# One hybrid trunk step on one core: eight buffers for the first modulation loads, layer 0's rotations stored from GpSimd's queue, and one of its four quarters of scan tables computed by GpSimd

## The chip, the cores and the metric

The kernel runs on one core of a Trainium2 chip. A core has five engines that each run their own list of instructions in order: TensorE (PE; its weight loads are shown apart as PEld), VectorE (DVE), ScalarE (ACT), GpSimd (POOL) and SyncE (SP). ACT, POOL and SP also issue DMA transfers (shown as ACTq, POOLq, SPq). An instruction waits for what it needs, and everything behind it on the same engine waits with it. The metric is the device time of one execution in microseconds (us); lower is better.

## The reference

The reference is one inference step of a two-layer trunk over 512 latent tokens and 128 context tokens, 1024 wide. Cut to what matters here:

```python
def trunk_layer(x, mod, p, ctx):
    shift1, scale1, gate1, shift2, scale2, gate2 = mod      # silu(cond) @ w_mod[l] + b_mod[l]
    h = modulate(x, shift1, scale1)                         # rms(x) * (1 + scale) + shift
    z = h @ p['w_in']
    u_ssm, c_q, ckv, k_rope, uv = split(z)
    y_a, h_re, h_im = mixer_ssm(u_ssm, h0_re, h0_im, p)     # S5 scan, both directions, 16 groups
    y_b = block_attention(q, k, v)                          # latent attention, 8 heads
    y_c = mixer_gmlp(uv, p)
    x = x + gate1 * merge_heads(y_a, y_b, y_c, p['w_out_norm'], p['w_out'])
    return x + gate2 * conv_ffn(modulate(x, shift2, scale2), p)

def ssm_direction(u, h0, ...):                              # one direction of mixer_ssm
    a_bar = exp(A * dt); b_bar = (a_bar - 1) / A * B
    h[t] = a_bar * h[t - 1] + b_bar * u[t]                  # complex, 64 states a group
    y[t] = real(C * h[t])
```

## The kernel before

The residual stream xT stays in SBUF, channels on the partitions, 642 token columns. Products of full precision are made of three passes: each weight tile is loaded raw, cast by ACT (whi, line 117) and its rest taken by DVE (wlo, line 118), and PE multiplies hi by hi, hi by lo and lo by hi.

At the start of layer 0, PE multiplies the condition by four blocks of w_mod (sixteen loads of 512 KB by SP, three shared buffers "raw", line 256; matmuls "mod", line 260). They give shift and scale. Then each half of the tokens is normalised and modulated (DVE nt L352 and hl L357, ACT hh L356) and multiplied by w_in ("win" and "wtok").

The scan is chunked by eight positions. It needs, for each layer and each of four quarters of the groups, tables in DRAM: WEd (state input), Qd (output), Wd (direct taps), and for all quarters together the rotations Td (powers of rho). `ssm_tables(l, q, ...)` computes a quarter: tiles B, Cr, CT, bb, bs, G, we, Q0, Q1, tm, with transposes and a tap product on PE and copies on ACT. `ssm_rotations` computes Td in parts of four columns, 42 element-wise products on GpSimd for a part (tile Tr, scratch tr). For layer 0 these run while norm and w_in run: rotations on GpSimd, four quarters of tables on DVE, all put in DRAM by SP's queue. For layer 1 both run on GpSimd during layer 0's FFN.

`scans` then goes over the quarters: `ssm_load` brings we, T, qt and tp back by GpSimd's queue; `ssm_quarter` makes E on PE and ACT, fills R on ACT (line 728), and on DVE does m = E*T (line 741), the scan H (749), m = H*T (751) and the states hq (758, 760) that PE multiplies by qt. The tiles E, R, m1, m2, H, T, we, qt, tp, hq and ys are single slots of the pool `ssm`; before the scans the rotations' tiles lie in the slots E, R, m1 and m2.

`params(l)` loads a layer's small vectors by GpSimd's queue, transposes them on PE (line 147, "pa") and copies them on DVE.

A scheduler that runs while the program is built fixes the order of each engine; nothing is reordered on the chip.

Of the kernel before, what the change touches and what calls it, by code (L numbers as in the profile page):

```python
# [10 lines left out]
F32 = mybir.dt.float32  # L11
# [8 lines left out]
D = 1024  # L20
# [3 lines left out]
NT = 642          # token columns: 512 latent, 2 zero, 128 context  # L24
CX = 514          # first context column
# [3 lines left out]
NS = 82           # scan slots per row  # L29
NC = 81           # chunk columns per row (64 latent, 1 gap, 16 context)  # L30

TOK = [0, 128, 256, 384, CX]     # first column of each token tile

# [14 lines left out]
class Trunk:  # L48
# [17 lines left out]
    def banks(self, pairs):  # L66
        """PSUM of one phase: six banks, as four single ones or two pairs of them."""
# [20 lines left out]
    # ---------------------------------------------------------------- helpers  # L88
    def complex_mul(self, eng, o_re, o_im, a_re, a_im, b_re, b_im, t):
        """o = a * b (o apart from a and b); t: two scratch APs of the result's shape."""  # L90
# [7 lines left out]
    def rsqrt(self, v, n):  # L98
        """v: [128, n] tile -> tile of 1/sqrt(v)."""
# [15 lines left out]
    def split(self, raw, hi, lo):  # L115
        """hi + lo == raw, each short enough for one float32r pass."""
        self.nc.scalar.copy(hi, raw)  # L117
        self.nc.vector.tensor_tensor(lo, raw, hi.bitcast(F32), op=OP.subtract)  # L118

    def wload(self, src, shape, pool=None, tags=("whi", "wlo"), bufs=5, into=None):  # L120
        """src: DRAM AP [128, a, b] (a*b <= 1024), or a list of (first index in a, AP)
        -> (hi, lo) views of that shape."""
# [22 lines left out]
    def tr(self, out, in_, k=128):  # L145
        """PE transpose of in_ ([k, m]) into out ([m, k])."""
        self.nc.tensor.transpose(out, in_, self.ident[:k, :k])

    # ---------------------------------------------------------------- constants and parameters
# [16 lines left out]
    def params(self, l):  # L166
        """Vectors of layer l with their index on the partitions."""
# [48 lines left out]
    def cond(self):  # L216
        """silu of both condition vectors, as 32-column stationary blocks."""
# [12 lines left out]
    def mod_blocks(self, l, blocks):  # L230
        """Blocks of 512 columns of the modulation of layer l; a generator of four steps a
        block and a last one."""
# [17 lines left out]
        for b in blocks:  # L250
            src = self.I["w_mod"][l, :, b * 512:(b + 1) * 512].rearrange("(k p) n -> p k n", p=128)
            ps = self.pz("mod")
            for kp in range(4):
                raw = self.wp.tile([128, 1024], F32, name=self.uid("raw"), tag="raw", bufs=3)
# [20 lines left out]
    # ---------------------------------------------------------------- residual in and out  # L275
# [32 lines left out]
    # ---------------------------------------------------------------- modulated norm  # L308
    def norm(self, pool, l, which, lo, hi, hh, hl):
        """The statistics at once; returns what does the rest."""  # L310
# [1437 lines left out]
```

## Time and profile before

| what | value |
|---|---|
| three runs | 1848.2, 1854.93, 1855.78 us (median 1854.93) |
| span of the profiled execution, first to last instruction | 1844.3 us |
| granted TensorE clock, mean over the span | 0.954 |
| PE busy | 1712.1 us, 93% |
| DVE busy | 1153.7 us, 63% |
| ACT busy | 680.5 us, 37% |
| GpSimd busy | 265.3 us, 14% |

The profiled execution's own time beside its span is not listed; the three timed runs lie 3.9 to 11.5 us above that span. Busy shares are means over very unlike stages: for most of the span PE is busy without a break, and in the first 270 us it is busy for 201.35.

### The profile page before, as it was taken

How to read it: one execution, taken by the hardware profiler on the slowest of the kernel's cores; microseconds unless marked ns; L12 is line 12 of the kernel's file. 1: busy time of each engine (PE TensorE's matmuls, PEld its weight loads, DVE VectorE, ACT ScalarE, POOL GpSimd, SP SyncE). 2: the span in 40 equal slices, each digit the busy share in tenths (PEclk: the TensorE clock that was granted, in tenths of full speed). 3: DMA queues.
4: the chain of work that ended last, by engine and by line, in shares of the span. 5: the costliest groups of instructions: out<-in, count | busy, mean ns of one | idle time of the engine just before them, and what ended most of it. 6: DMA issues, size and time to landing. Idle time of an engine off the chain costs nothing.

```text
span 1844.3 us, 28301 instructions
## 1 busy us (share of the span) xinstructions
PE 1712.1 (93%) x10864; PEld 1497.3 (81%) x10864; DVE 1153.7 (63%) x2461; ACT 680.5 (37%) x1210; POOL 265.3 (14%) x720
## 2 busy tenths in 40 slices
PE   6777889999999999999999988999989999999998
PEld 2665754559799899999998875455979999999998
DVE  5867784667764546466567578566777464655564
ACT  3342453532451414234244355353335132332241
POOL 3920300000024040439000120000000000000000
PEclk7886989999999999999999978999989999999999
DMA  7464534402433424134121633440222131321221
GB/s 222 135 163 123 140 110 159 138 1 69 126 119 100 151 65 126 54 98 125 54 89 66 159 107 105 156 141 1 69 69 92 32 107 44 94 82 45 81 81 58
DMA packets 201895, 182.44 MB, mean 99 GB/s; under 512 B 33438, under 2 KB 162780, under 8 KB 201760
## 3 DMA queue, kind: packets, MB, share of 16 engines
q1 hardware_dynamic: 182224, 163.57, 29.3%
q0 software_dynamic: 5104, 14.62, 2.7%
q10 hardware_dynamic: 14432, 2.44, 0.7%
q8 instruction: 86, 1.41, 0.3%
q14 instruction: 49, 0.40, 0.1%
HBM read 161.94 MB, written 18.64 MB: 98 GB/s over the span
## 4 chain that ended last, share of the span: by engine, by line
PE 74%; DVE 9%; DMA 8%; ACT 4%; POOL 3%; issue 2%; ACTq 0%; SPq 0%; DVEq 0%; POOLq 0%
PE up L141 11%; PE up L143 11%; PE up L142 11%; PE dn L142 5%; PE dn L141 5%; PE dn L143 5%; PE mod L260 4%; DMA raw<-w_mod 3%; PE o L1278 3%; PE wo L141 1%; PE wo L143 1%; PE wo L142 1%; PE s L1258 1%; PE mx L1239 1%; PE win L141 1%
## 5 line engine op out<-in xcount | busy, mean ns | idle before, releaser
L141 PE MATMUL up<-hh,whi 128*128 128x322 f32 x1408 | 436.5, 315 | 9.5 <-ACT hh L356 8.7
L142 PE MATMUL up<-hl,whi 128*128 128x322 f32 x1408 | 439.6, 313 | 2.1 <-DVE hl L357 1.9
L143 PE MATMUL up<-hh,wlo 128*128 128x322 f32 x1408 | 440.6, 314 | 0.4 <-DVE wlo L118 0.4
L141 PEld LDWEIGHTS up<-hh,whi 128*128 128x128 f32 x1408 | 266.2, 191 | 22.3 <-issue 11.0
L142 PEld LDWEIGHTS up<-hl,whi 128*128 128x128 f32 x1408 | 268.5, 191 | 2.9 <-DVE hl L357 2.9
L143 PEld LDWEIGHTS up<-hh,wlo 128*128 128x128 f32 x1408 | 267.9, 190 | 1.7 <-issue 1.0
L118 DVE TENSOR_TENSOR wlo<-raw,whi 128x1024 fp32r<-128x1024 f32 (+1 forms) x116 | 143.5, 1240 | 142.1 <-ACT whi L117 133.4
L142 PE MATMUL dn<-glo,dh 128*128 128x322 f32 (+1 forms) x704 | 217.7, 311 | 0.0
L143 PE MATMUL dn<-gh,dl 128*128 128x322 f32 (+1 forms) x704 | 217.4, 310 | 0.0
L141 PE MATMUL dn<-gh,dh 128*128 128x322 f32 (+1 forms) x704 | 208.8, 310 | 0.1
L1492 DVE SCALAR_TENSOR_TENSOR xT<-dn,mod,xT 128x320 f32<-128x320 f32 (+2 forms) x288 | 112.1, 435 | 129.9 <-PE dn L143 129.7
L117 ACT CAST whi<-raw 128x1024 fp32r<-128x1024 f32 (+1 forms) x116 | 120.4, 1041 | 157.1 <-PE up L142 63.9
L1523 ACT ACTIVATE cv<-up,prm,cw 128x321 f32<-128x321 f32 x88 | 54.2, 620 | 247.0 <-PE up L143 243.3
L143 PEld LDWEIGHTS dn<-gh,dl 128*128 128x128 f32 x704 | 132.9, 189 | 0.0
L142 PEld LDWEIGHTS dn<-glo,dh 128*128 128x128 f32 x704 | 132.7, 188 | 0.0
L141 PEld LDWEIGHTS dn<-gh,dh 128*128 128x128 f32 x704 | 130.3, 189 | 0.6 <-ACT gh L117 0.6
L260 PE MATMUL mod<-raw,sT 128*32 128x512 f32 x384 | 93.9, 672 | 20.1 <-DMA raw<-w_mod 17.2
L1524 DVE SCALAR_TENSOR_TENSOR cv<-up,cw,cv 128x320 f32<-128x320 f32 x88 | 48.3, 549 | 73.2 <-ACT cv L1523 73.0
L118 DVE TENSOR_TENSOR dl<-raw,dh 128x1024 fp32r<-128x1024 f32 x44 | 56.6, 1286 | 35.3 <-ACT dh L117 35.2
L1241 DVE TENSOR_REDUCE nml<-mx 128x1 f32<-128x640 f32 x64 | 51.1, 818 | 26.3 <-PE mx L1239 26.0
L117 ACT CAST dh<-raw 128x1024 fp32r<-128x1024 f32 x44 | 46.2, 1049 | 48.3 <-DMA raw<-ffn_w_down 44.9
L141 PE MATMUL wo<-yh,whi 128*128 128x322 f32 (+1 forms) x192 | 59.9, 317 | 1.8 <-ACT yh L117 1.0
(468 smaller groups left out, 3316.0 us busy)
## 6 DMA issues: line engine op xcount, KB each, us to landing
raw<-w_mod SPq DMA_DIRECT2D x96, 512.0 KB, 4.0
raw<-ffn_w_up SPq DMA_DIRECT2D x88, 512.0 KB, 4.0
raw<-ffn_w_down SPq DMA_DIRECT2D x44, 512.0 KB, 3.3
raw<-w_in SPq DMA_DIRECT2D x10, 512.0 KB, 4.8
WEd<-we SPq DMA_DIRECT2D x16, 256.0 KB, 2.1
Qd<-Q SPq DMA_DIRECT2D x32, 128.0 KB, 1.9
we<-WEd POOLq DMA_DIRECT2D x8, 512.0 KB, 4.1
qt<-Qd POOLq DMA_DIRECT2D x8, 512.0 KB, 5.0
```

Of the source, the lines that this page charges most:

```text
L117: self.nc.scalar.copy(hi, raw)
L118: self.nc.vector.tensor_tensor(lo, raw, hi.bitcast(F32), op=OP.subtract)
L141: mm(ps, wh, xh, start=start, stop=False)
L142: mm(ps, wh, xl, start=False, stop=False)
L143: mm(ps, wl, xh, start=False, stop=stop)
L260: nc.tensor.matmul(ps[c:c + 32, :], self.sT[:, k, :], rv[:, j, :], start=k < 4, stop=k >= 4)
L1239: mm(pb[:, o, :320], qh[i][:96, tt * 128:(tt + 1) * 128], kh[i][:96, o * 320:(o + 1) * 320], start=True, stop=True)
L1241: V.tensor_reduce(nm[:, tt:tt + 1], pb[:, :, :320], axis=AX.XY, op=OP.max, negate=True)
L1278: mm(pb[i * 64:(i + 1) * 64, 0], Vt[:, kt, 2 * p + i], Ps[i][kt], start=kt == 0, stop=kt == 4)
L1492: self.nc.vector.scalar_tensor_tensor(self.xT[:, m, a:b], po[:, a - lo:b - lo], self.modcol(l, gi, m, c), self.xT[:, m, a:b], op0=OP.mult, ...
L1523: A.activation(z[:, 0:321], po[:, 0:321], AF.Identity, bias=b, scale=c1)
L1524: V.scalar_tensor_tensor(z[:, 1:321], po[:, 0:320], c0, z[:, 1:321], op0=OP.mult, op1=OP.add)
```

## The change

1. The four modulation blocks ahead of layer 0 load into a pool of their own, `pre`, of eight buffers, instead of the three shared ones. The pool lies on the right side, where `params(0)` had its rows.
2. `params(1)` moves from right behind the modulation to just before layer 0's scans.
3. Quarters 0, 1, 2 of layer 0's tables stay on DVE. Quarter 3 is computed by GpSimd, in the slots that the scans use later (tm0 in E, tm1 in R, G in m1, we in m2, Q0 in H, Q1 in T, and so on). Its puts go by GpSimd's queue.
4. Layer 0's rotations are made in four parts one after the other, in one tile (slot hq) and one scratch tile (slot ys), behind the scan input; all Td stores go by GpSimd's queue. hq is allocated when the scans begin.
5. Layer 1's tables are put away by GpSimd's queue too, and its rotations are made in two parts of eight columns instead of four of four.

The diff, cut to its core:

```diff
-    def mod_blocks(self, l, blocks):
+    def mod_blocks(self, l, blocks, pool=None):
...
-                raw = self.wp.tile([128, 1024], F32, name=self.uid("raw"), tag="raw", bufs=3)
+                raw = (pool or self.wp).tile([128, 1024], F32, name=self.uid("raw"), tag="raw",
+                                             bufs=8 if pool else 3)
...
-    def ssm_tables(self, l, q, pool, E):
+    def ssm_tables(self, l, q, pool, E, tags={}, ps_of=None):
...
+        ps_of = ps_of or self.pz
+        put = nc.gpsimd if E is nc.gpsimd else nc.sync
...
-            return pool.tile(list(sh), F32, name=self.uid(s), tag=s, bufs=bufs)
+            return pool.tile(list(sh), F32, name=self.uid(s), tag=tags.get(s, s), bufs=bufs)
...
-            nc.sync.dma_start(out=self.WEd[l][q][:, d].rearrange("p e r n -> p (e r n)"), in_=we)
+            put.dma_start(out=self.WEd[l][q][:, d].rearrange("p e r n -> p (e r n)"), in_=we)
...
-                nc.sync.dma_start(out=self.Qd[l][q][:, d, h], in_=Qv[:, h, :, o:o + 128])
+                put.dma_start(out=self.Qd[l][q][:, d, h], in_=Qv[:, h, :, o:o + 128])
...
-                nc.sync.dma_start(out=self.Wd[l][q][:, :, gq].rearrange("j c n -> c j n"), in_=src)
+                put.dma_start(out=self.Wd[l][q][:, :, gq].rearrange("j c n -> c j n"), in_=src)
...
-    def ssm_rotations(self, l, pool, E, tags):
-        for d in range(2):
-            for g0 in (0, 4):
-                c0 = l * 16 + d * 8 + g0
-                T = pool.tile([128, 4, 2, NS], F32, name=self.uid("Tr"), tag=tags[g0 // 4], bufs=1)
-                tm = [pool.tile([128, 4 * 32], F32, name=self.uid("tr"), tag=tags[2 + i], bufs=1)
...
-                    nc.sync.dma_start(
-                        out=self.Td[l][g0 // 2 + q][:, d].rearrange("p e r n -> p (e r n)"),
+    def ssm_rotations(self, l, pool, E, parts, tags=("Tr", "tr")):
+        N = 16 // parts
+        for p0 in range(0, 16, N):
+            c0 = l * 16 + p0
+            T = pool.tile([128, N, 2, NS], F32, name=self.uid("Tr"), tag=tags[0], bufs=1)
+            tm = pool.tile([128, 2, N * 32], F32, name=self.uid("tr"), tag=tags[1], bufs=1)
...
+            for i in range(0, N, 2):
+                d, q = divmod(p0 + i, 8)
+                nc.gpsimd.dma_start(
+                    out=self.Td[l][q // 2][:, d].rearrange("p e r n -> p (e r n)"),
...
-        hq = ssm.tile([128, 2, 2, 2, NS], F32, name=self.uid("hq"), tag="hq")
         if l == 0:
-            self.ssm_rotations(0, ssm, nc.gpsimd, ("E", "R", "m1", "m2"))
...
         U = self.ssm_input(l, ssm, uT)
+        if l == 0:
+            tags = {"tm0": "E", "tm1": "R", "G": "m1", "we": "m2", "Q0": "H", "Q1": "T",
+                    "B": "we", "Cr": "qt", "CT": "tp", "bb": "bbg", "bs": "bsg"}
+            for q in (3,):
+                self.ssm_tables(0, q, ssm, nc.gpsimd, tags, lambda s: self.pb(s)[:, 0])
+            self.ssm_rotations(0, ssm, nc.gpsimd, 4, ("hq", "ys"))
 
         def scans(tables):
+            hq = ssm.tile([128, 2, 2, 2, NS], F32, name=self.uid("hq"), tag="hq")
...
-            for q in range(4):
+            for q in (0, 1, 2):
                 self.ssm_tables(0, q, tb, V)
             tb_ctx.close()
+            self.params(1)
             scans(None)
...
-            mix = self.begin_layer(0, self.mod_blocks(0, (2, 0, 3, 1)))
-            self.params(1)
+            with tc.tile_pool(name="pre", bufs=1, side="right") as pre:
+                mix = self.begin_layer(0, self.mod_blocks(0, (2, 0, 3, 1), pre))
...
-                    hooks[4] = [lambda: self.ssm_rotations(l + 1, tb[0], nc.gpsimd,
-                                                           ("T0", "T1", "tm0", "tm1"))]
+                    hooks[4] = [lambda: self.ssm_rotations(l + 1, tb[0], nc.gpsimd, 2)]
```

The scheduler draws each engine's order anew. Three places matter later.

SP, the start, before: the first modulation loads stand right behind the loads of x.

```order
8 L283 DMA raw_396<-x_prompt 128x1024
9 L256 DMA raw_423<-w_mod 128x2x512
10 L256 DMA raw_427<-w_mod 128x2x512
11 L256 DMA raw_431<-w_mod 128x2x512
```

SP, the same place, of the change:

```order
8 L284 DMA raw_396<-x_prompt 128x1024
9 L134 DMA raw_685<-w_in 128x8x128
10 L134 DMA raw_692<-w_in 128x8x128
11 L886 DMA raw_823<-w_in 128x2x288
12 L257 DMA raw_426<-w_mod 128x2x512
13 L257 DMA raw_430<-w_mod 128x2x512
```

Three loads of w_in now stand ahead of the first of w_mod, and that first one waits until PE has transposed the rows of `params(0)`, because its buffer lies where they were.

ACT, end of the second half's norm, before: the fill of R for the first scan (two rows, slot R still holding a rotation part) stands between the norm's last hh.

```order
104 L356 ACTIVATE hh_415<-nt_985,mod_91 128x192
105 L356 ACTIVATE hh_415<-nt_989,mod_91 128x128
106 L728 COPY R_2029<-r_266 128x328 x2
107 L356 ACTIVATE hh_415<-nt_993,mod_91 128x192
108 L356 ACTIVATE hh_415<-nt_997,mod_91 128x128
```

ACT, of the change, where R is filled now: 66 rows behind the norm's last hh, beside the gMLP's scaling of v (line 1106) and the tap copies of quarter 3 (we_1081) and quarter 2 (we_1949).

```order
188 L1106 ACTIVATE v_1386<-v_1386,rs_y_240_1540 128x256 x5
189 L598 COPY we_1912<-we_1907 128x512
190 L731 COPY R_2029<-r_266 128x328 x2
191 L637 COPY we_1081<-tap_1060 128x240
192 L637 COPY we_1949<-tap_1928 128x240
193 L720 COPY E_2005<-e_2006 128x4x81
```

So no hh stands behind the fill of R any more.

POOL, of the change, the end of quarter 3 (Q_198) and the fourth rotation part (Tr_1232), the loads tp, T and we of the scans among them, and the first row of `params(1)`:

```order
242 L611 TENSOR_TENSOR Q_198_1047<-tm_188_986,tm_189_987 64x288 x2
243 L696 DMA tp_2003<-Wd_295 128x512
...
257 L95 TENSOR_TENSOR Tr_1232<-Tr_1232,tr_1233 128x4x8
258 L692 DMA T_1999<-Td_287 128x656
...
262 L646 DMA Wd_298<-we_1081 16x8x128 x4
...
267 L174 MEMSET rows_1960 13x128
...
299 L95 TENSOR_TENSOR Tr_1232<-Tr_1232,tr_1233 128x4x18
300 L96 TENSOR_TENSOR Tr_1232<-Tr_1232,tr_1233 128x4x18
301 L668 DMA Td_289<-Tr_1232 128x328
```

Before, GpSimd had nothing but memsets, small copies and loads behind the rotations; now quarter 3, four Wd puts and ten loads of `params(1)` (between rows 267 and 280) stand there as well, and the last Td store is row 302.

DVE, of the change, ahead of the first scan: the finish of quarter 3's taps (we_1081), the gMLP's gate (gt, yc) and quarter 2's taps (we_1949), then the scan's first product.

```order
346 L638 SCALAR_TENSOR_TENSOR we_1081<-id_80,dcol_1058,we_1081 128x16
347 L1113 TENSOR_TENSOR gt_1557<-gm_1555,gvb_339 128x320
...
351 L638 SCALAR_TENSOR_TENSOR we_1949<-id_80,dcol_1926,we_1949 128x16
...
356 L744 TENSOR_TENSOR m_320_2036<-E_2005,T_1999 128x656
```

Row 346 needs the tap product that PE makes of GpSimd's Q_198; before, the taps of all quarters came from DVE's own tables.

## Rows read from the trace of the kernel before

**Rows 1.** Windows: stretch, us, busy (count) PE PEld DVE ACT POOL, PEclk, DMA share, GB/s.

```profile
640.00:680.00 40.00, 40.00 (x296) 39.63 (x295) 17.95 (x38) 7.96 (x15) 22.19 (x42) 1.00 0.33 92
...
sum 400.00, PE 399.48 PEld 389.57 DVE 219.90 ACT 130.60 POOL 129.75; mean PE 39.95 PEld 38.96 DVE 21.99 ACT 13.06 POOL 12.98
```

**Rows 2.** Windows of the first 170 us by stage.

```profile
20.00:55.00 35.00, 26.35 (x95) 6.86 (x93) 27.68 (x147) 8.57 (x17) 12.93 (x51) 0.64 0.74 239
55.00:80.00 25.00, 17.84 (x110) 17.14 (x109) 21.03 (x53) 12.40 (x24) 25.00 (x80) 0.80 0.49 138
...
99.70:109.10 9.40, 1.31 (x8) 0.82 (x7) 0.28 (x2) 1.22 (x4) 3.72 (x15) 0.67 0.42 119
109.10:138.00 28.90, 25.16 (x205) 24.12 (x205) 21.81 (x72) 15.09 (x49) 1.30 (x4) 0.91 0.73 185
138.00:170.00 32.00, 23.74 (x167) 18.50 (x167) 25.19 (x70) 9.75 (x27) 0.84 (x4) 0.69 0.48 130
```

**Rows 3.** Timeline from 99.4 us: start, length, what [idle before <-releaser].

```profile
107.88 0.46 ACT L728 COPY R<-r 128x328 f32<-128x328 f32 x1 [11.19 <-DMA Td<-Tr]
...
109.10 0.42 DVE L357 SCALAR_TENSOR_TENSOR hl<-nt,mod,hh 128x192 fp32r<-128x192 f32 x1 [9.12 <-ACT hh L356]
...
109.12 0.61 PE L899 MATMUL wtok<-wth,hh 128*128 128x288 f32 x1 [8.11 <-ACT hh L356]
```

**Rows 4.** The chain that ended last, one piece: start, us, what.

```profile
102.94 4.85 DMA Td<-Tr
```

**Rows 5.** SP's timeline at the start: sixteen issues in a row.

```profile
14.44 35.88 SPq L256 DMA_DIRECT2D raw<-w_mod  x16
```

**Rows 6.** Windows: a stretch while w_mod streams.

```profile
26.00:32.00 6.00, 3.35 (x9) 0.37 (x9) 4.26 (x18) 2.73 (x6) 0.29 (x1) 0.65 0.86 282
```

**Rows 7.** DVE's timeline: the first product of the first half's norm.

```profile
54.81 0.54 DVE L352 SCALAR_TENSOR_TENSOR nt<-xT,mod,nbc 128x320 f32<-128x320 f32 x1
```

**Rows 8.** DVE's groups, 54 to 73.5 us: count, busy us, mean ns, idle before.

```profile
L118 DVE TENSOR_TENSOR wtl<-raw,wth 128x576 fp32r<-128x576 f32 x4 | 3.0, 746 | 0.0
L118 DVE TENSOR_TENSOR wlo<-raw,whi 128x1024 fp32r<-128x1024 f32 x2 | 2.6, 1278 | 0.0
```

**Rows 9.** DVE's groups, 110 to 170 us.

```profile
L608 DVE TENSOR_TENSOR Q<-tm,tm 64x288 f32<-64x288 f32 x24 | 10.8, 452 | 0.6
L604 DVE TENSOR_TENSOR tm<-pw,CT 128x288 f32<-128x288 f32 x12 | 5.4, 454 | 1.3 <-ACT CT L554 1.1
L605 DVE TENSOR_TENSOR tm<-pw,CT 128x288 f32<-128x288 f32 x12 | 5.4, 451 | 0.0
...
L92 DVE TENSOR_TENSOR tm<-pw,bb 128x256 f32<-128x256 f32 x6 | 2.5, 421 | 0.0
```

**Rows 10.** DVE's timeline: last table row, the first scan's product, its states.

```profile
169.76 0.24 DVE L635 SCALAR_TENSOR_TENSOR we<-id,dcol,we 128x16 f32<-128x16 f32 x1 [4.91 <-ACT we L634]
170.29 0.84 DVE L741 TENSOR_TENSOR m<-E,T 128x656 f32<-128x656 f32 x1 [0.29 <-POOL E L724]
...
180.21 1.13 DVE L758 TENSOR_TENSOR hq<-m 64x164 f32<-64x164 f32 x4
```

**Rows 11.** GpSimd's timeline: first and last of the four parts' 168 products.

```profile
47.64 0.24 POOL L91 TENSOR_TENSOR Tr<-Tr,rho 128x4 f32<-128x4 f32 x1
...
102.20 0.32 POOL L96 TENSOR_TENSOR Tr<-Tr,tr 128x72 f32<-128x72 f32 x1
```

**Rows 12.** GpSimd in layer 0's FFN: the same product of two successive parts.

```profile
828.32 0.20 POOL L92 TENSOR_TENSOR tr<-Tr,rho 128x4 f32<-128x4 f32 x1
...
837.54 0.21 POOL L92 TENSOR_TENSOR tr<-Tr,rho 128x4 f32<-128x4 f32 x1
```

**Rows 13.** GpSimd's timeline: one DMA issue.

```profile
127.44 0.54 POOL L693 DMA_DIRECT2D tp<-Wd  x1 [16.92 <-DMA Qd<-Q]
```

**Rows 14.** DVE's groups, 73 to 99 us, beside GpSimd's rotations.

```profile
L608 DVE TENSOR_TENSOR Q<-tm,tm 64x288 f32<-64x288 f32 x8 | 3.8, 479 | 0.2
```

More of the change, by code (lines that the diff above doesn't have):

```diff
@@ L550, in ssm_tables @@
                         in_=I["ssm_c_" + nm][l, d, g:g + 2].rearrange("g c p -> (g c) p"))
-        ps = self.pz("ct")
+        ps = ps_of("ct")
         self.tr(ps[:, :128], Cr)
@@ L588, in ssm_tables @@
                              [v4(x, 8) for x in tm])
-            ps = self.pz("we")
+            ps = ps_of("we")
             for e in range(2):
@@ L613, in ssm_tables @@
             for h in range(2):
-                nc.sync.dma_start(out=self.Qd[l][q][:, d, h], in_=Qv[:, h, :, o:o + 128])
+                put.dma_start(out=self.Qd[l][q][:, d, h], in_=Qv[:, h, :, o:o + 128])
         dcol = t("dcol", [128, 1])
         nc.gpsimd.memset(dcol, 0.0)
-        ps = self.pz("tap")
+        ps = ps_of("tap")
         for h in range(2):
@@ L642, in ssm_tables @@
                               ap=[list(src.ap[0]), [-16, 8], [1, 128]])
-                nc.sync.dma_start(out=self.Wd[l][q][:, :, gq].rearrange("j c n -> c j n"), in_=src)
-    def ssm_rotations(self, l, pool, E, tags):
+                put.dma_start(out=self.Wd[l][q][:, :, gq].rearrange("j c n -> c j n"), in_=src)
+    def ssm_rotations(self, l, pool, E, parts, tags=("Tr", "tr")):
         nc = self.nc
-        for d in range(2):
-            for g0 in (0, 4):
-                c0 = l * 16 + d * 8 + g0
-                T = pool.tile([128, 4, 2, NS], F32, name=self.uid("Tr"), tag=tags[g0 // 4], bufs=1)
-                tm = [pool.tile([128, 4 * 32], F32, name=self.uid("tr"), tag=tags[2 + i], bufs=1)
-                      for i in range(2)]
-                nc.gpsimd.memset(T[:, :, 0, 0:1], 1.0)
-                nc.gpsimd.memset(T[:, :, 1, 0:1], 0.0)
-                for j in range(7):
-                    b = 1 << j
-                    n = min(b, NS - b)
-                    sh = [128, 4, n]
-                    r_re, r_im = (bc(self.rho[:, j, r, c0:c0 + 4, None], sh) for r in range(2))
-                    x = [a[:, :4 * n].rearrange("p (g n) -> p g n", g=4) for a in tm]
-                    self.complex_mul(E, T[:, :, 0, b:b + n], T[:, :, 1, b:b + n],
-                                     T[:, :, 0, 0:n], T[:, :, 1, 0:n], r_re, r_im, x)
-                for q in range(2):
-                    nc.sync.dma_start(
-                        out=self.Td[l][g0 // 2 + q][:, d].rearrange("p e r n -> p (e r n)"),
-                        in_=T[:, 2 * q:2 * q + 2].rearrange("p e r n -> p (e r n)"))
@@ new lines, in ssm_rotations @@
+        N = 16 // parts
[3 more added lines that the diff above has]
+            tm = pool.tile([128, 2, N * 32], F32, name=self.uid("tr"), tag=tags[1], bufs=1)
+            nc.gpsimd.memset(T[:, :, 0, 0:1], 1.0)
+            nc.gpsimd.memset(T[:, :, 1, 0:1], 0.0)
+            for j in range(7):
+                b = 1 << j
+                n = min(b, NS - b)
+                sh = [128, N, n]
+                r_re, r_im = (bc(self.rho[:, j, r, c0:c0 + N, None], sh) for r in range(2))
+                x = [tm[:, i, :N * n].rearrange("p (g n) -> p g n", g=N) for i in range(2)]
+                self.complex_mul(E, T[:, :, 0, b:b + n], T[:, :, 1, b:b + n],
+                                 T[:, :, 0, 0:n], T[:, :, 1, 0:n], r_re, r_im, x)
+            for i in range(0, N, 2):
+                d, q = divmod(p0 + i, 8)
+                nc.gpsimd.dma_start(
+                    out=self.Td[l][q // 2][:, d].rearrange("p e r n -> p (e r n)"),
+                    in_=T[:, i:i + 2].rearrange("p e r n -> p (e r n)"))
```

## The prediction, made before the change was run

> **What bounds the kernel now.** I read the busy times by stage first, then the idle times and their releasers, then the chain that ended last. In layer 0's FFN, where layer 1's tables and rotations are made, PE is busy for 399.48 of 400 us [rows 1]: what GpSimd and its queue do there lies beneath PE, so the change's part for layer 1 is costed at nothing. Its cover is large: the tables are needed only when layer 1 begins, and GpSimd is busy for 129.75 of those 400 us.
>
> The time to be had lies in the first 180 us. From 20 to 55 us the sixteen modulation loads set the pace, from 55 to 80 DVE and GpSimd share the work, and from 99.7 to 109.1 nearly everything stands still: in 9.4 us PE works for 1.31 and DVE for 0.28 [rows 2]. The timeline says why. ACT's fill of R waited 11.19 us for Td<-Tr, since R's slot held a rotation part that had to be stored first; the norm's last hh stood behind it, and DVE waited 9.12 us and PE 8.11 us for that [rows 3]. The store itself is on the chain with 4.85 us [rows 4]. From 109.1 to 170 us DVE is busy for 47.0 of 60.9 us and PE for 48.9, at a granted clock that falls from 0.91 to 0.69 [rows 2]: neither engine is full, they wait for each other.
>
> **The change part by part.**
>
> *Modulation loads.* Before, they are issued from 14.44 to 50.3 us [rows 5]. Now three w_in loads (2 x 512 KB and 288 KB, 1.34 MB) go ahead and the first w_mod waits for the transposes of params(0). The fastest rate that the trace shows here is 282 GB/s [rows 6], the mean 239 [rows 2]; I take 250. The three loads are 5.4 us at that, so w_mod begins at about 20. Sixteen loads (8.39 MB) and three more of w_in between them (0.88 MB) take 33 to 39 us, 37 at 250: the last lands at 53 to 59 us, I take 57. Before, the norm could begin at 54.81 [rows 7]. More buffers thus do not end the modulation earlier: they keep the queue full, but the queue also carries w_in. What they bring comes later: the lower parts of w_in, 3.0 and 2.6 us of DVE [rows 8], no longer stand inside the first half's norm. Gain: 5.6 less 2 to 3, so 3 us (0 to 6).
>
> *The stall.* R is now filled behind all hh, so its 9.4 us go; I take 9. What hides the new fill is quarter 3 on GpSimd, whose scratch lies in R; that wait is costed below.
>
> *A quarter of tables off DVE.* On DVE it is 8 Q at 452 ns, 8 tm at 453 and 12 products for G at about 420 [rows 9]: 3.6 + 3.6 + 5.0 = 12.2 us, and small ones. Of 109.1 to 170 us, DVE's 47.0 would become 35. PE's 48.9 us there would be 25.16 x 0.91 + 23.74 x 0.69 = 39 at full clock, so this stage cannot shrink by more than about 15; at nothing, if PE sets it at its old clock. I take 12, as the quarter's own chain (tables, transposes, copies, store) goes with its work.
>
> Without GpSimd the sum is 3 + 9 + 12 = 24 us: the first scan's states, now at 180.21 [rows 10], would start at 156.
>
> *GpSimd.* It begins when the modulation's buffers are free, at about 58 us instead of 47.64 [rows 11]. Ahead of its row 242 (the end of quarter 3) stand 3.1 rotation parts, the quarter, 14 DMA issues, three waits for a part's stores before its tile is written again, and waits for PE and ACT. A part takes 54.9 / 4 = 13.7 us beside a busy DVE [rows 11] and 9.2 in the FFN [rows 12]; I take 12.5, nearer to the first, since DVE is as busy here. A quarter is 22.2 us in the FFN [rows 1]; with the parts' ratio (1.49) it would be 33; I take 26.6. An issue is 0.54 us [rows 13]. So: 39 + 26.6 + 7.6 + 5 for the stores + 5 for the other waits = 83 us (60 to 97), and row 242 is done at 141. DVE's row 346, and behind it the gMLP's gate and the scan's product, wait for the taps that PE makes of it. Then 23 more issues (12.4 us; ten are params(1), whose first memset waits for quarter 2's last puts), the rest of the fourth part (9), memsets (2) and the landing of the last stores (2): 25.5 us. The states hq, whose slot held the rotations, can be written at 166.5. That is later than the 156 that DVE and PE alone would need, so GpSimd decides: 180.2 - 166.5 = 13.7, say 14 us. The bounds: at 60 us of work the 24 stands (30 with every upper end), at 97 the gain is nothing.
>
> The scans, attention and everything behind are the same work, so the 14 us reach the end. On the profiled span that is 1844.3 - 14 = 1830.3; the median of the runs is 10.6 above that span, and I keep that: 1854.93 - 14 = 1841 us.
>
> *GpSimd beside DVE.* With GpSimd's rotations beside it, a Q product on DVE took 479 ns [rows 14], and 452 without [rows 9]: 6%, at most 2 us over the stretch, left out of the sum. GpSimd pays far more, 13.7 against 9.2. The Trainium skill, page "SBUF — State Buffer", section "Who interferes with whom", speaks against the change: a VectorE instruction with two SBUF inputs and a GpSimd instruction that reads SBUF lock each other out for a whole instruction. In this trace nearly all of that falls on GpSimd; the rule taken evenly is the third rival below.
>
> **The rivals.**
>
> 1. *GpSimd is hidden* (0.22). Row 242 comes before 130 us and DVE and PE set the time: 24 us, 1831. For it: parts at 9.2 as in the FFN. Against: DVE was nowhere idle while the parts took 13.7.
>
> 2. *GpSimd ends too late; slower* (0.14). The place is DVE's row 346, the wait for quarter 3's taps, with the gate and the scan behind it, and then hq. It decides when row 242 is done after 180.2 - 25.5 = 154.7 us, that is when GpSimd needs 97 us and not 83. Parts at 13.7 (42.5), the quarter at 33, issues 7.6, stores 6 and 15 of other waits are 104 us: row 242 at 162, hq at 188, 8 us late: 1863. For it: GpSimd, ACT and PE hand quarter 3 back and forth, and each is in order.
>
> 3. *DVE is held up by GpSimd* (0.12). If each of some 60 products with two inputs in SBUF (about half of the 53 and 72 that rows 2 count for two of the stretches) lost half of a GpSimd product (0.25 us), DVE would be 15 us longer and the gain 24 - 15 = 9: 1846. Against it: rows 14.
>
> 4. *The gain is given back* (0.14). The scans' loads stand in GpSimd's queue among rotations and params(1), and DVE's copies of params(1) stand between the scan and hq; if these and the later modulation cost what the stall gave, some 4 us remain: 1851.
>
> My forecast (GpSimd decides, but earlier than now; 0.38) has its own range of 1832 to 1853.
>
> **How the numbers follow.** A measurement of this kernel can tell about 0.5% (9.3 us) from no change. Faster by more: 0.30 of the forecast's 0.38, rival 1 and half of rival 3, 0.58. Within 0.5%: the forecast's rest (0.08), half of rival 3, 0.12 of rival 4 and 0.02 of rival 2, 0.28. Slower: 0.14. The range, 1824 to 1862, holds rival 1 with its upper bounds (30 us) and most of rival 2's near side; it leaves out about 0.13.
>
> **What would show it.** Right: no idle time of DVE before an hl near 100 us; R's fill waiting for GpSimd and nothing behind it that the norm needs; the first nt within 53 to 59 us and no wlo or wtl inside the first half's norm; DVE idle before the taps of quarter 3 or the states with GpSimd or its DMA as releaser; GpSimd busy without a break from 58 to about 165 us; the FFN as long as before. Wrong: the first scan's product waiting for nothing of GpSimd's (rival 1), hq after 180 us (rival 2), Q products on DVE above 600 ns (rival 3), or hq early and attention beginning no earlier than before (rival 4).

## The result, and the profile after

The changed kernel takes 1831.07 us (median of 4 runs, 1829.74 to 1833.83) against 1851.57 for the kernel before (4 runs, 1845.65 to 1855.78): a ratio of 0.989, interval 0.9864 to 0.9916. That is 20.5 us less; the forecast was 14 less. The profiled span fell by 14.3 us, from 1844.3 to 1830.0. That this is the 14 of the sum is chance, as the last experiment below shows: the first profile of the kernel before fell on a quick execution.

Busy times by stage, the stretches of [rows 2]:

```profile
20.00:55.00 35.00, 23.21 (x92) 6.11 (x93) 33.01 (x155) 13.71 (x29) 1.96 (x14) 0.80 0.89 303
55.00:80.00 25.00, 23.66 (x156) 22.56 (x154) 19.64 (x52) 10.57 (x28) 24.75 (x82) 0.93 0.12 24
99.70:109.10 9.40, 6.18 (x51) 5.78 (x49) 9.27 (x12) 3.23 (x8) 9.39 (x17) 1.00 0.82 215
109.10:138.00 28.90, 17.73 (x132) 16.03 (x132) 23.90 (x58) 10.24 (x29) 22.83 (x45) 0.77 0.69 183
138.00:170.00 32.00, 30.37 (x266) 26.40 (x266) 24.85 (x50) 14.72 (x37) 26.39 (x67) 0.94 0.53 149
```

The columns are those of [rows 2]: stretch, us, busy (count) of PE, PEld, DVE, ACT and POOL, PEclk (the granted TensorE clock), DMA share, GB/s. From 20 to 55 us the transfers run at 303 GB/s instead of 239, and DVE is nearly full: busy for 33.01 of 35 us, against 27.68. From 55 to 80 PE works 23.66 us instead of 17.84. The standstill from 99.7 to 109.1 is gone: DVE is busy for 9.27 of 9.4 us, GpSimd for 9.39.

SP's timeline at the start, where [rows 5] had sixteen loads of w_mod in one row:

```profile
13.78 3.88 SPq L134 DMA_DIRECT2D raw<-w_in  x2
18.91 0.37 SPq L886 DMA_DIRECT2D raw<-w_in  x1
19.65 12.97 SPq L257 DMA_DIRECT2D raw<-w_mod  x10
...
35.87 3.75 SPq L257 DMA_DIRECT2D raw<-w_mod  x4
```

The first w_mod is issued at 19.65, as forecast (20), the last by 39.6 instead of 50.3.

DVE's timeline: first and last product of the norm, the last table row (of quarter 2), the scan's product m and its states, for [rows 7, 10]:

```profile
53.48 0.99 DVE L353 SCALAR_TENSOR_TENSOR nt<-xT,mod,nbc 128x320 f32<-128x320 f32 x2
...
94.41 0.34 DVE L358 SCALAR_TENSOR_TENSOR hl<-nt,mod,hh 128x128 fp32r<-128x128 f32 x1
...
147.49 0.32 DVE L638 SCALAR_TENSOR_TENSOR we<-id,dcol,we 128x16 f32<-128x16 f32 x1 [0.24 <-ACT we L637]
...
152.47 0.84 DVE L744 TENSOR_TENSOR m<-E,T 128x656 f32<-128x656 f32 x1 [1.32 <-POOL E L727]
...
173.31 0.32 DVE L761 TENSOR_TENSOR hq<-m 64x164 f32<-64x164 f32 x1 [2.19 <-DMA Td<-Tr]
```

m comes 17.8 us earlier than before, hq only 6.9. The states wait 2.19 us for the rotations' last store, as forecast; m itself waits 1.32 us for GpSimd's copy into E.

GpSimd's timeline: its first rotation product, the end of quarter 3 (row 242), the waits behind it, the last stores, for [rows 11]:

```profile
53.47 0.20 POOL L91 TENSOR_TENSOR Tr<-Tr,rho 128x4 f32<-128x4 f32 x1
...
138.22 1.85 POOL L611 TENSOR_TENSOR Q<-tm,tm 64x288 f32<-64x288 f32 x2
...
147.43 0.59 POOL L692 DMA_DIRECT2D T<-Td  x1 [2.56 <-PE tap L635]
...
154.03 0.20 POOL L174 MEMSET rows<- 13x128 f32 x1 [1.59 <-DMA Wd<-we]
...
168.07 1.15 POOL L668 DMA_DIRECT2D Td<-Tr  x2 [0.30 <-POOL Tr L96]
```

DVE's groups, 73 to 152 us, for [rows 9, 14]; count, busy us, mean ns:

```profile
L611 DVE TENSOR_TENSOR Q<-tm,tm 64x288 f32<-64x288 f32 x24 | 13.8, 575 | 0.6
L608 DVE TENSOR_TENSOR tm<-pw,CT 128x288 f32<-128x288 f32 x12 | 7.2, 600 | 0.0
L607 DVE TENSOR_TENSOR tm<-pw,CT 128x288 f32<-128x288 f32 x12 | 7.0, 581 | 1.1 <-ACT CT L557 1.1
L94 DVE TENSOR_TENSOR tm<-pw,bb 128x256 f32<-128x256 f32 x5 | 5.0, 991 | 0.0
```

The same products took 452, 451, 454 and about 420 ns before. The means hide how the time is lost. DVE's view of the tiles tm and Q over the same stretch gives the shortest, the median and the longest in ns:

```profile
L611 DVE TENSOR_TENSOR Q<-tm,tm x24: 445/461/1021, 76.7 to 143.4; 64x288 f32<-64x288 f32 x24
L94 DVE TENSOR_TENSOR tm<-pw,bb x5: 418/434/3152, 82.5 to 136.9; 128x256 f32<-128x256 f32 x5
```

Most products are as quick as before. The mean of 991 ns comes from one product of 3.15 us among five. It began at 105.66, and four products of quarter 3 ran on GpSimd under it, one right after the other. Ten more table products took 0.85 to 1.25 us each, all begun between 109 and 139 us, while GpSimd worked on quarter 3.

### The profile page after: what moved, and what is told of

Same layout as the page of the kernel before. It is cut to its first block, busy times and chain, and to the rows that moved or that the text cites. A ratio compares the mean times of both kernels' runs of the same rounds, so it can differ in the third digit from the quotient of the medians.

```text
span 1830.0 us, 28203 instructions
## 1 busy us (share of the span) xinstructions
PE 1708.6 (93%) x10864; PEld 1499.7 (82%) x10864; DVE 1158.5 (63%) x2421; ACT 681.7 (37%) x1210; POOL 311.4 (17%) x738
## 4 chain that ended last, share of the span: by engine, by line
PE 75%; DVE 10%; DMA 8%; ACT 4%; issue 2%; POOL 1%; ACTq 1%; DVEq 0%; POOLq 0%
PE up L141 11%; PE up L143 11%; PE up L142 10%; PE dn L142 5%; PE dn L143 5%; PE dn L141 5%; PE mod L261 3%; DMA raw<-w_mod 3%; PE o L1287 3%; PE wo L141 1%; PE wo L143 1%; PE wo L142 1%; DVE wlo L118 1%; DMA raw<-ffn_w_up 1%; PE s L1267 1%
## 5 line engine op out<-in xcount | busy, mean ns | idle before, releaser
L118 DVE TENSOR_TENSOR wlo<-raw,whi 128x1024 fp32r<-128x1024 f32 (+1 forms) x116 | 147.4, 1272 | 155.2 <-ACT whi L117 146.5
L141 PE MATMUL dn<-gh,dh 128*128 128x322 f32 (+1 forms) x704 | 208.9, 310 | 2.3 <-DVE xT L1501 1.5
L261 PE MATMUL mod<-raw,sT 128*32 128x512 f32 x384 | 89.7, 642 | 21.7 <-DMA raw<-w_mod 19.8
```

The costliest lines, as they stand in the source:

```text
L141: mm(ps, wh, xh, start=start, stop=False)
L261: nc.tensor.matmul(ps[c:c + 32, :], self.sT[:, k, :], rv[:, j, :], start=k < 4, stop=k >= 4)
```

## The experiments

Two questions: which part of the change brings the gain, and does GpSimd decide through the states hq, as the prediction has it, or does the time follow something earlier, the scan's first product m, whatever hq does (the rival)? A third theory, that DVE pays for GpSimd's quarter, is told from both by the durations of DVE's own products. The diffs are cut to their core.

The times of all kernels, with four moments of their profiles: v, ACT's last copy of the gMLP's input out of PE's wtok (line 947 of the changed kernel); m, the scan's first product; hq, its first states; wo, PE's first matmul of layer 0's output projection. Medians of 4 to 12 runs each, ratio to the kernel before on the same chip; that kernel's medians there lie between 1851.57 and 1855.13, so that a difference of medians in us can be off by some 3.

| kernel | v | m | hq | wo | wo - m | wo - hq | median | ratio (interval) |
|---|---|---|---|---|---|---|---|---|
| before | 131.7 | 170.3 | 180.2 | 398.0 | 227.7 | 217.8 | 1851.57 | 1 |
| before, profiled again | 134.2 | 172.2 | 182.1 | 403.2 | 231.1 | 221.1 | 1852.85 | 1.0004 (0.9984 to 1.0024) |
| after | 124.9 | 152.5 | 173.3 | 382.2 | 229.8 | 208.9 | 1831.07 | 0.989 (0.9864 to 0.9916) |
| 1 eight buffers alone | 124.7 | 186.8 | 196.7 | 416.2 | 229.4 | 219.5 | 1871.1 | 1.0097 (1.0066 to 1.0128) |
| 2 rotation slots alone | 137.7 | 169.3 | 178.9 | 403.2 | 233.9 | 224.3 | 1855.98 | 1.0021 (1.0003 to 1.0039) |
| 3 quarter 3 on DVE | 118.2 | 160.8 | 170.5 | 392.9 | 232.1 | 222.4 | 1837.24 | 0.9919 (0.9892 to 0.9947) |
| 4 params(1) early | 132.4 | 183.6 | 194.2 | 409.5 | 225.9 | 215.3 | 1866.09 | 1.0088 (1.0056 to 1.0121) |
| 5 three buffers | 127.1 | 166.5 | 173.6 | 392.9 | 226.4 | 219.3 | 1845.57 | 0.997 (0.9954 to 0.9986) |
| 6 own slot | 145.1 | 152.7 | 160.9 | 387.2 | 234.5 | 226.3 | 1839.76 | 0.9953 (0.9933 to 0.9973) |
| 7 buffers, late params(1) | 133.6 | 168.3 | 178.3 | 397.8 | 229.5 | 219.5 | 1854.27 | 1.0018 (1.0 to 1.0036) |
| 8 params(1) behind the mixers | 124.5 | 152.8 | 164.9 | 386.0 | 233.2 | 221.1 | 1833.43 | 0.9899 (0.9873 to 0.9925) |
| 9 U behind w_in | 132.6 | 172.5 | 182.5 | 403.1 | 230.6 | 220.6 | 1857.64 | 1.0009 (0.999 to 1.0028) |
| 10 short rotations | 118.5 | 141.4 | 150.8 | 370.9 | 229.5 | 220.1 | 1825.84 | 0.9841 (0.9816 to 0.9865) |
| 11 two parts | 150.2 | 164.5 | 171.4 | 395.3 | 230.8 | 223.9 | 1844.83 | 0.9943 (0.9921 to 0.9964) |

**1. Eight buffers alone.** The kernel before with the pool `pre` and nothing else; params(1) stays right behind the modulation.

```diff
...
-            mix = self.begin_layer(0, self.mod_blocks(0, (2, 0, 3, 1)))
+            with tc.tile_pool(name="pre", bufs=1, side="right") as pre:
+                mix = self.begin_layer(0, self.mod_blocks(0, (2, 0, 3, 1), pre))
             self.params(1)
```

> The kernel before with only the eight modulation buffers. Theory A (the steps of the prediction): w_in's lower parts leave the first half's norm, the second half's norm begins about 8 us earlier (68.7 against 77.1 us in the changed kernel), but the rotations still lie in the scan's slots and DVE still computes four quarters; and the order drawn here also has R's fill behind the norm, so that the stall should be gone too: 8 to 14 us faster, 1838 to 1844. Theory B (the quarter on GpSimd and the rotations' slots bring nearly all): at most 4 us faster, 1848 or more.

It was slower by about 1%: theory A is out, and theory B names no loss. GpSimd's timeline, then the waits (total, times, longest), 53 to 80 us:

```profile
61.51 0.20 POOL L174 MEMSET rows<- 13x128 f32 x1 [3.88 <-PE mod L261]
```

```profile
POOL uT L868 <- PE pa L147: 10.2, 1, 10.2
...
DVE cw L198 <- PE pa L147: 4.6, 1, 4.6
...
PE pa L147 <- DMA rows<-q_norm: 3.4, 1, 3.4
```

The rows of params(1) get the memory of `pre`, so their memset waits for the last modulation matmul, ten loads follow, and PE, DVE and GpSimd wait for these in the middle of the first norm.

**2. Rotation slots alone.** The kernel before with the rotations of parts 4 and 5 of the change: those of layer 0 in hq and ys, those of layer 1 in two parts, Td stored by GpSimd's queue. Layer 0's are still written ahead of the scan input, and layer 1's tables still go by SP's queue.

```diff
...
-            self.ssm_rotations(0, ssm, nc.gpsimd, ("E", "R", "m1", "m2"))
+            self.ssm_rotations(0, ssm, nc.gpsimd, 4, ("hq", "ys"))
...
```

> The kernel before with only the rotations moved: one tile in hq's slot, four parts one after the other, stores by GpSimd's queue; three buffers, four quarters on DVE. Theory A: the stall of 9.4 us before 109 us goes, and nothing else changes: 7 to 10 us faster, 1842 to 1845. Theory B (the stall only hid other waits: DVE's four quarters set the time up to the first scan): under 4 us faster.

The stall is gone (the norm ends at 100.0 us, not 110.2), yet m stays at 169.3 and the time is not shorter. SP's timeline, then the waits from 100 to 170 us:

```profile
108.64 8.07 SPq L677 DMA_DIRECT2D U<-Ud  x8
117.13 0.39 SPq L884 DMA_DIRECT2D raw<-w_in  x1
```

```profile
PE wtok L899 <- DVE wtl L118: 8.2, 2, 4.5
```

The last w_in load of line 884 stands behind the eight U loads in SP's queue, and PE waits for it. Experiment 9 takes this cover away.

**3. Quarter 3 on DVE.** The changed kernel with all four quarters on DVE: buffers, rotations and the late params(1) stay.

```diff
-            for q in (3,):
-                self.ssm_tables(0, q, ssm, nc.gpsimd, tags, lambda s: self.pb(s)[:, 0])
...
-            for q in (0, 1, 2):
+            for q in range(4):
```

> The changed kernel with quarter 3 of the tables back on DVE in its own pool, everything else as changed. Theory A: what the quarter takes from DVE (12 us) is partly given back, since GpSimd's chain sets the first scan's states and DVE's products run slower beside GpSimd; so 3 to 9 us slower than the changed kernel, 1834 to 1840. Theory B (the quarter on GpSimd is the main gain): 12 us or more slower, 1843 or above. Theory C (it brings nothing, GpSimd's lateness and the slower DVE eat it all): within 2 us of the changed kernel.

The norm ends at 87.3 us, 7.5 before that of the changed kernel, but m comes 8.4 us later. DVE's groups from 73 to 152 us:

```profile
L611 DVE TENSOR_TENSOR Q<-tm,tm 64x288 f32<-64x288 f32 x28 | 13.1, 468 | 0.8
L607 DVE TENSOR_TENSOR tm<-pw,CT 128x288 f32<-128x288 f32 x15 | 7.2, 482 | 0.3
```

With the rotations alone on GpSimd, DVE's products cost 468 and 482 ns in the mean, not 575 and 581. With the quarter on GpSimd the norm ends 7.5 us later and the stretch behind it is 15.8 us shorter (from the norm's end to m: 73.6 us here, 57.7 in the changed kernel). A part of both is only work that changes place: in the norm's second half DVE makes 67 instructions in the changed kernel, 55 here, since more table products stand among those of the norm.

**4. params(1) early.** The changed kernel with params(1) where it was.

```diff
             tb_ctx.close()
-            self.params(1)
             scans(None)
...
+            self.params(1)
```

> The changed kernel with params(1) back behind the modulation, as before, so that its ten loads are out of GpSimd's queue at the first scan. Theory A (GpSimd's queue sets when the states can be written): its ten issues (5.4 us) and the wait for quarter 2's puts leave the path, the first states come 5 to 8 us earlier, and the time falls by 3 to 8 us, to 1823 to 1828. Theory D (the states' lateness is hidden by other work of PE and DVE): within 2 us of the changed kernel.

The same wait as in experiment 1, at the same place: the memset of the rows waits 3.88 us for PE, uT 10.5 us, and the first nt starts at 59.07. Both theories were wrong. The late params(1), which I costed only as issues in GpSimd's chain and as a part of rival 4, is worth 35 us here: only with it does `pre` pay.

**5. Three buffers.** The changed kernel without `pre`.

```diff
-            with tc.tile_pool(name="pre", bufs=1, side="right") as pre:
-                mix = self.begin_layer(0, self.mod_blocks(0, (2, 0, 3, 1), pre))
+            mix = self.begin_layer(0, self.mod_blocks(0, (2, 0, 3, 1)))
```

> The changed kernel with the modulation's first blocks in the three shared buffers again; params(1) late, rotations and quarter 3 as changed. Theory A: the lower parts of w_in stand inside the first half's norm again and the second half begins 8 us later; of that some 4 us are left at the end, since GpSimd sets the first states: 2 to 6 us slower than the changed kernel, 1833 to 1837. Theory B (the buffers matter only in that they force params(1) late; the late params(1) is what helps): within 2 us of the changed kernel. If the whole gain hangs on the eight buffers: 1845 or above.

Of the 20.5 us, 14.5 are gone. The windows of its first two stages:

```profile
20.00:55.00 35.00, 23.84 (x95) 6.79 (x95) 30.62 (x148) 8.87 (x21) 13.22 (x49) 0.86 0.79 245
55.00:80.00 25.00, 18.72 (x111) 17.76 (x110) 20.23 (x43) 11.44 (x24) 21.49 (x60) 0.80 0.35 97
```

The first nt comes at 52.6, no later than with eight buffers; but from 55 to 80 us, w_in still streams (97 GB/s, 24 with eight) and PE has 18.72 us of work, not 23.66. From the first half's first nt to the second half's first, the kernels with eight buffers take 14.4 to 17.7 us, those with three 22.0 to 24.5. Not all of the 14.5 us is of this kind: the second half begins 5.9 us later than in the changed kernel, m comes 14.0 later. The rest arises behind the norm, where the order is drawn anew (DVE waits 4.56 us for the put Wd<-we just ahead of m), and was not taken apart.

**6. Own slot.** The changed kernel with the rotations' tile in a slot of its own, so that hq need not wait for their stores.

```diff
-            self.ssm_rotations(0, ssm, nc.gpsimd, 4, ("hq", "ys"))
+            self.ssm_rotations(0, ssm, nc.gpsimd, 4, ("rT", "ys"))
```

> The changed kernel with the rotations' tile in a slot of its own, so that the first states need not wait for the last rotation to be stored; GpSimd's work is the same. Theory A (the states wait for GpSimd through that slot): the 2.2 us that DVE waited for Td<-Tr goes and the states come 3 to 8 us earlier, 2 to 6 us faster, 1825 to 1829. Theory D (the slot is hidden; DVE has other work in front of the states): within 2 us of the changed kernel.

DVE's timeline:

```profile
152.69 0.84 DVE L744 TENSOR_TENSOR m<-E,T 128x656 f32<-128x656 f32 x1 [3.27 <-POOL E L727]
...
160.94 1.37 DVE L761 TENSOR_TENSOR hq<-m 64x164 f32<-64x164 f32 x4
```

hq comes 12.4 us earlier, m does not, and the kernel is 8.7 us slower than the changed one, which neither theory allowed. What makes it slower was not settled by a run of its own: v is 20 us later (ACT's order puts R's fill, which waits for GpSimd's Q, between the copies), the gMLP's gate, which waits for v, ends on DVE at 167.2 us instead of 151.1, partly behind hq, and wo - m is at the upper end. So this run moves more than hq; experiment 8 is the cleaner test.

**7. Eight buffers and late params(1).** Experiment 1 with params(1) in front of the scans.

```diff
             tb_ctx.close()
+            self.params(1)
             scans(None)
...
```

> The kernel before with the eight buffers and params(1) just before the scans; rotations in their old slots and stores on SP's queue, four quarters on DVE. Theory E (eight buffers alone cost 18 us because params(1) had to wait for their memory and held up PE, DVE and GpSimd; with params(1) moved they gain): first norm product at 53 to 55 us instead of 60, 1836 to 1845, so 25 us or more better than the eight buffers alone. Rival (the eight buffers cost for another reason, such as the order of w_in among w_mod): 1855 or above.

The loss of experiment 1 is gone and the first norm product comes at 53.8 us, as theory E has it, but there is no gain. The waits from 90 to 168 us:

```profile
PE wtok L900 <- ACT wth L117: 10.3, 1, 10.3
```

The norm is no longer stalled (it ends at 91.9 us), but the rotations' stores now hold up SP's queue: two of Td's stand at 112.49 between U's loads, the w_in load that PE needs comes behind them at 116.34, and m is where it was with the stall.

**8. params(1) behind the mixers.** The changed kernel with ten loads fewer between quarter 3 and the rotations' last part.

```diff
-            self.params(1)
...
                 fh, fl, second = self.mixers(l, M, n1, N, hh, hl, self.mod_blocks(l, range(4, 12)))
+                if l == 0:
+                    self.params(1)
```

> The changed kernel with params(1) behind the mixers of layer 0: its ten loads come behind all of the scans' loads in GpSimd's queue, and its copies on DVE no longer stand ahead of the first states. Theory A: the last rotation stores come 6 us earlier (the issues and the wait for quarter 2's puts), the first states at about 166 to 168 instead of 173.3, and the time falls by 3 to 7 us, to 1824 to 1828. Theory D (what stands behind the states sets the time): within 2 us.

DVE's timeline:

```profile
152.80 0.95 DVE L744 TENSOR_TENSOR m<-E,T 128x656 f32<-128x656 f32 x1 [0.75 <-POOL E L727]
...
164.95 0.31 DVE L761 TENSOR_TENSOR hq<-m 64x164 f32<-64x164 f32 x1
```

Again hq is earlier (8.4 us), m is not, and the time is that of the changed kernel. Here v (124.5) and the gate's end (152.0) also are where they were.

**9. U behind w_in.** Experiment 2 with U's loads behind the last w_in load.

```diff
...
-        U = self.ssm_input(l, ssm, uT)
+        U = self.ssm_input(l, ssm, uT) if l > 0 else None
...
         wt = token_load(928, 256)
+        if l == 0:
+            U = self.ssm_input(l, ssm, uT)
```

> The rotations' slots alone (as in the second run), with the loads of U written behind the last loads of w_in, so that SP issues the last one of w_in ahead of U. There PE had waited 8.2 us for wtl, since that load stood behind the eight of U on SP. Theory S (SP's order ate the stall's 9.4 us): v comes 7 to 9 us earlier and the first scan's product with it, the time falls by 5 to 9 us against the second run, 1847 to 1851. Theory M (DVE's four quarters of tables set when the first scan's product starts, and FFN follows it at a fixed distance): v comes earlier, but the product stays at 166 to 170 us and the time within 4 us of the second run, 1852 to 1860.

v comes 5.1 us earlier than in experiment 2 and m no earlier: behind the norm, the four quarters of tables on DVE remain, and m follows their last row (170.7).

**10. Short rotations.** The changed kernel with GpSimd's load cut: it leaves out the last six of the seven doublings of layer 0's rotations, so that the scans read zeros for most of Td and the kernel does not compute the reference; only its times are of use.

```diff
...
-            for j in range(7):
+            for j in range(7 if l else 1):
```

> The changed kernel with layer 0's rotations cut to the first of seven doublings (the rest of Td is zero; the work left out is six sevenths of the rotations' products, nothing else). Theory M with contention (GpSimd's products slow DVE's tables by about 10 us between 95 and 152 us, and the first scan's product sets the end): the tm products on DVE fall from about 590 to 480 ns or less outside quarter 3's own time, the first product comes at 138 to 146 us instead of 152.5, and the time falls to 1815 to 1826. Theory H (the first states, which wait for the last rotation's store, set the end): the states come 15 us or more earlier and the time falls by 12 us or more even if the first product stays. Theory D (neither): within 4 us of the changed kernel.

DVE's timeline and its groups from 73 to 152 us:

```profile
141.43 0.84 DVE L746 TENSOR_TENSOR m<-E,T 128x656 f32<-128x656 f32 x1 [2.08 <-POOL E L729]
...
150.81 1.13 DVE L763 TENSOR_TENSOR hq<-m 64x164 f32<-64x164 f32 x4
```

```profile
L611 DVE TENSOR_TENSOR Q<-tm,tm 64x288 f32<-64x288 f32 x24 | 13.5, 564 | 0.6
L608 DVE TENSOR_TENSOR tm<-pw,CT 128x288 f32<-128x288 f32 x11 | 6.0, 547 | 0.0
```

m is 11.0 us earlier, hq 22.5, wo 11.3: the output projection follows m. The span is 7.7 us shorter, the median 5.2. tm falls only to 547 ns, not to the 480 of theory M, and Q on DVE still costs 564 ns in the mean (median 454), so their slowness comes from the quarter's products on GpSimd much more than from the rotations. Quarter 3 ends on GpSimd at 122.7 us instead of 140.1; that this reaches m shows that GpSimd is not hidden either.

**11. Two parts.** The changed kernel with layer 0's rotations in two parts of eight columns.

```diff
-            self.ssm_rotations(0, ssm, nc.gpsimd, 4, ("hq", "ys"))
+            self.ssm_rotations(0, ssm, nc.gpsimd, 2, ("hq", "ys"))
```

> The changed kernel with layer 0's rotations in two parts of eight columns instead of four of four: half as many products on GpSimd, twice as long, and all rotations ahead of quarter 3's output products. Theory M: quarter 3 ends 5 to 12 us earlier on GpSimd (its taps no longer wait for), the first scan's product starts at 145 to 151 us and the time is 1824 to 1831, at best the fastest of all. If GpSimd's products take as long per element, and the order drawn here costs what it gains: within 3 us of the changed kernel.

The waits of DVE, 73 to 170 us:

```profile
DVE gt L1113 <- PE gm L1110: 7.4, 2, 6.2
```

The kernel is 13.8 us slower than the changed one, against both expectations: quarter 3 ends on GpSimd at 139.8 us, against 140.1, not 5 to 12 us earlier. v is 25 us later, since on ACT it now stands behind quarter 3's taps; the gMLP's gate waits for it, m behind the gate, and the time follows m. Longer instructions on GpSimd also hold DVE up for longer: beside rotation products of 128x256, three of DVE's table products between 97 and 100 us took 831 to 953 ns; beside those of 128x128, in the kernel before, none took more than 675.

**12. The kernel before, profiled again.**

> The kernel before, unchanged, profiled a second time. Its first profiled execution has a span of 1844.3 us, while its runs here have medians of 1852 to 1855 us and spread from 1844 to 1862. Theory A (the first profile fell on a quick execution): the second has a span of 1848 to 1858, the first scan's product m again near 170 and wo near 398 (both within 3), and what is longer lies behind wo, at a lower granted clock there; then 14.3 us of the 20 between the medians are seen in the two profiles, and the rest is this spread. Theory B (the time outside the span is longer in timed runs of this kernel): the span is again near 1844 and the run some 8 us over it. Theory C (the first 180 us vary): m lies 5 us or more away from 170.3, and the milestones of the first profile are no measure for the others. Ratio 1.000 within 0.003.

DVE's timeline:

```profile
172.15 0.84 DVE L741 TENSOR_TENSOR m<-E,T 128x656 f32<-128x656 f32 x1 [0.30 <-POOL E L724]
...
182.08 1.12 DVE L758 TENSOR_TENSOR hq<-m 64x164 f32<-64x164 f32 x4
```

The span is 1853.6 us, 9.3 more than in the first profile of the same program, and the run 1855.4, 1.8 over its span (as in every other run that lists both). Of the 9.3 us, 1.9 lie ahead of m, 3.4 between m and wo and 4.0 behind; wo is 5.3 us later, more than theory A allowed. So the first profile fell on one of the quickest executions, and a difference of a few us between two single profiles says little.

## Why the prediction was right, and where its steps were not

*The total.* 1831 lies in the range, on the side forecast, 10 us below the value. It lies 1 us outside the range of the forecast's own mechanism (1832 to 1853) and on the value of rival 1, so that the right total owes something to luck. Nearly all of the 10 us is one term: I kept 10.6 us between the profiled span and the median. The execution itself takes 1.8 us more than its span; the rest was the distance of a quick execution from the median. 1830.3 + 1.8 would have been 1832. But against an ordinary execution of the kernel before the gain is 20 us, not 14, so the sum was also short, and its terms were off in both directions.

*Modulation loads: mis-sized.* I gave them 3 us: 5.6 for w_in's lower parts, which leave the first half's norm, less 2 to 3 for a later start, with the transfers at 250 GB/s. They run at 303 (experiment 5: 245 with three buffers), and the norm starts 1.3 to 1.8 us sooner, not later. The lower parts did leave it (between 55 and 80 us DVE makes none), and the stretch between the halves is 7.1 to 9.3 us shorter, not 5.6. Together it is 8.4 us against the first profile, 11.1 against the second. Experiment 5 puts the buffers' worth at 14.5 us of the time, with the reservation made there.

*The stall: right as a stall, not as a gain of its own.* 9 us forecast. In experiment 2, where only the rotations are changed, it is 23.6 us from the second half's first nt to the norm's end instead of 33.1, 9.5 less; but m comes only 1.0 us sooner and the time does not fall. In the changed kernel the same stretch is 26.0 us, 7 less, and R is filled at 140 with no hh behind it.

*Quarter 3: right in what it takes off DVE, wrong in what DVE pays.* 12 us forecast, 15.8 measured behind the norm (experiment 3 against the changed kernel), with work that changed place in it. The bounds that I put beside the 12 do not follow from the rows: 60.9 us less the 39 of PE at full clock leaves room for 22 us, less the 48.9 at its old clock for 12, not 15 and nothing. And I left at most 2 us for GpSimd beside DVE. The four groups above, at their counts, cost 3.0 + 1.8 + 1.5 + 2.9 = some 9 us more than at the old durations, nearly all of it behind the norm, between 105 and 140 us. The norm's own 7.5 us are something else, in part more table products inside it and in part hl (627 ns against 446 in experiment 3 for the second half's 192-column form). The net is 8.4 us at m and 6.2 between the medians; the intervals of the two ratios overlap. Rival 3 thus was half true, though Q's mean stayed below the 600 ns that I had named for it. The rule of the Trainium skill (page "SBUF — State Buffer", section "Who interferes with whom") that I set against rows 14 stands better than I allowed, and the trace agrees with it: a few products are held up while one or more of GpSimd's run, the longest takes 3.15 us, and most are hardly touched (medians of 434 to 475 ns). What misled me is that [rows 14] show DVE beside rotations alone, many of them short.

*"GpSimd decides, through hq": the step that failed.* The chain itself was well sized up to quarter 3's end: row 242 done at 140.1, forecast 141 (it began 4.5 us sooner and took 86.6 us, not 83). hq came at 173.3, forecast 166.5, for the waits for PE's taps and for a Wd store and the scans' own copies stand between the rows. But hq does not set the time. In experiments 6 and 8 it is 12.4 and 8.4 us earlier, with m in the same place to within 0.4 us, and neither wo nor the time is earlier (experiment 6 also delays the gate, experiment 8 does not). The profile's chain of the work that ended last, in the changed kernel, says the same and keeps GpSimd in it; start, us, what:

```profile
138.22 0.89 POOL Q L611
...
147.43 0.59 POOL T L692
...
149.56 1.58 POOL Wd L646 x3
...
151.63 5.14 DMA we<-WEd
156.90 0.78 PE e L716 x16
```

From the end of quarter 3 it goes over PE's taps and through GpSimd's queue (the load T, four puts of Wd, the load of the next quarter's table) to PE, and not over the first quarter's hq. So GpSimd does stand on the path, as forecast, but ahead of the place that I named. The chain is inferred from releasers, and no run changed these queue entries alone.

The times of the other kernels bear on the same question. In the table's 14 profiles, wo follows m at 225.9 to 234.5 us while m moves over 45 us, and it follows hq less closely, at 208.9 to 226.3. The median less m lies between 1676 and 1687 us for all thirteen kernels. What the table cannot separate is m itself from what is ready with it (the gate, the tables' last rows, the loads behind m): I take it for the moment at which the serial work ahead of the scans is done, which is an inference. While hq waits PE and DVE have other work (138 to 170 us: PE busy for 30.37 of 32 us in the profile after, 23.74 in [rows 2]).

*The rivals.* Rival 1 (GpSimd hidden, 1831) names the right time with the wrong reason: row 242 came 10 us past its condition, m was released by GpSimd's copy into E, and experiment 10 shows that the rotations' load still costs 11 us at m. Rival 2 did not happen. Rival 4 did, but in the parts: the stall's gain was given back in experiments 2 and 7. It was kept when the buffers, the late params(1) and the rotations' slots stood together, with quarter 3 still on DVE (experiment 3: 0.9919, some 15 of the 20 us). *Layer 1's part* cost nothing, as forecast: from wo to the end it is 1447.8 us, against 1446.3 and 1450.4 in the two profiles of the kernel before.

*Left open.* The order that the scheduler chooses is redrawn by every edit, and wo - m and the stretch behind wo (1442.3 to 1456.4) vary by some 9 and 14 us among the kernels; the two profiles of one program already differ by 3.4 and 4.0 there. Smaller differences between single kernels, such as experiment 6's slowness, are not explained here.

## What to carry to other kernels

Look for the one moment at which the serial part ends and see whether the time follows it; a wait in front of something else (here the states) may be long and cost nothing while PE has other work. Try parts together and one by one: here the eight buffers alone, the same with the late params(1), and the rotations' move alone gained nothing, the first lost 1% through memory that passes on to the next tile in need of it, and the three together gained 0.8%. And compare a forecast with the median through the time that belongs to the profiled execution itself.

## What was not expected of the hardware

- With up to eight loads of 512 KB outstanding the transfers of the first stage ran at 303 GB/s, with three at 239 and 245 in the same stretch.
- The slowing of DVE by GpSimd depends on what GpSimd runs: in the mean 4 to 6% beside rotations (468 and 482 ns for 452 and 454), 27 to 33% over the stretch with a quarter of tables (575 to 600). It falls on few products: Q's median there is 461 ns, its longest 1021, and one product of another kind took 3152 instead of some 420.
- Executions of one program, the kernel before, spread from 1841.33 to 1861.82 us over all its runs here, on several chips; the two that were profiled, 9.3 us apart, had clocks of 0.954 and 0.955.
